# The opening of a diffusion layer: a conditioning product on four column strips, and squares summed by TensorE

## The chip, the cores and the metric

The kernel runs on one core of a Trainium2 chip. The metric is the device time of one execution in microseconds; for each version the median of its runs is compared. "The profile" is one execution recorded by the hardware profiler.

## The reference

One layer of a diffusion backbone over 512 latent tokens and 256 context tokens of 1024 features, all in float32. The layer is a feed-forward block, a token mixer (differential attention beside a short convolution) and a second feed-forward block. Only the beginning matters here:

```python
def rms_norm(x, g):
    xf = x.astype(jnp.float32)
    y = xf * lax.rsqrt(jnp.mean(xf * xf, axis=-1, keepdims=True) + EPS)
    return (y * g.astype(jnp.float32)).astype(x.dtype)

def modulate(x, shift, scale):
    return x * (1.0 + scale) + shift

def adaln(cond, w_mod, b_mod):
    m = jax.nn.silu(cond) @ w_mod + b_mod
    return jnp.split(m, N_MOD, axis=-1)

def swiglu(x, w_gate, w_up, w_down):
    return (jax.nn.silu(x @ w_gate) * (x @ w_up)) @ w_down

def ffn_sublayer(h, mods, pre_g, post_g, w_gate, w_up, w_down):
    shift, scale, gate = mods
    y = swiglu(modulate(rms_norm(h, pre_g), shift, scale), w_gate, w_up, w_down)
    return h + 0.5 * gate * rms_norm(y, post_g)
```

Two conditioning vectors (one for the latent tokens, one for the context) go through the same 1024 x 9216 matrix. Before the first gate and up products (1024 x 2816 each) can start, the kernel needs the first two of its nine parts, shift and scale, and one over the root mean square of every token.

## The kernel before

Features lie on partitions, tokens along the free axis. The 1024 features are 8 blocks `d` of 128 rows; the 2816 hidden features are 22 chunks `f`. A float32 product is mostly made as three float32r products of parts: `hi` (a cast by ScalarE, L64) and `lo` (a subtraction on VectorE or GpSimd, L69), so that `wx` (L94) issues hi x hi, hi x lo and lo x hi. A plain float32 product on TensorE shows as two records of the profile. All loads of the opening go out on one queue, SP's. The order on each engine is laid down by a planner at build time; it follows the order of the program text closely, with small swaps.

The opening (L236 to L374) runs in these steps:

- **Loads**, in order: the conditioning columns of blocks 0 to 2 (`load_mod`, L251, two halves of 512 KB for a block, 8 buffers), the latent tokens (8 x 256 KB), the context tokens (8 x 128 KB), the gate and up weights of hidden chunk 0 (2 x 512 KB, L271), and the conditioning columns of blocks 3 to 7.
- **Conditioning product** of a block (`mod_mm`): the two vectors are the stationary operand, the 256 columns (shift and scale of the block) move past, in 8 products over the 1024 rows. Blocks 0 to 3 (`NPLAIN = 4`) are made in plain float32 with a stationary operand of 4 columns. For blocks 4 to 7 `mod_split` first splits the columns into parts (two casts by ScalarE, a subtraction on VectorE and one on GpSimd), and 16 float32r products are made with 128 stationary columns, of which four hold the parts of the vectors.
- `mod_row` (L299) copies the resulting rows (4 x 256) out of PSUM; `mod_pick` turns them into columns with two small products against `pick`, which also adds the rows of the parts; `mod_col` (L310, L312) adds the bias and the gain.
- **Squares**: `sqadd` (L146) squares a block of tokens on ScalarE and adds it to one of two accumulators on VectorE or GpSimd. At the end `rstd_steps` (L109) makes four products for the latent tokens and two for the context, one for each 128 tokens, against a single column of ones; then comes the root (ScalarE), the reciprocal (VectorE), and a product of ones with a diagonal matrix for each 128 tokens (L123), which spreads the result over all partitions in PSUM: `pbl`, `pbc`.
- **Modulation** (`mod_x`, through `modulate`, L157): for the latent tokens and for the context each a multiplication on VectorE (L161, reading `pbl` or `pbc` in PSUM), a shift with a cast on ScalarE (L164) and the low part on VectorE (L165).
- **Gate and up products of chunk 0** (`gate_up_open`, L128): block by block, twelve products for each `d`, into four banks of PSUM. In the loop over blocks 3 to 7 each round has one conditioning product, the split of the next block's columns, the modulation of an earlier block, twelve gate and up products of that block, and the selection of the new block; the last three blocks follow.

After the opening, chunks 1 and on run through `gate_up1`: two loads of 512 KB, two splits, and 96 products for the two kinds of tokens. Between chunks VectorE sums the remaining conditioning products (`mod_unit`, L439), whose loads use the same queue and the same four buffers `wraw` as the weights.

Of the kernel before, what the change touches and what calls it, by code (L numbers as in the profile page):

```python
# [16 lines left out]
P = 128  # L17
DM = 1024
# [13 lines left out]
NFIRST = 3  # L32
NPLAIN = 4
# [8 lines left out]
class Builder:  # L42
# [51 lines left out]
    def wx(self, outs, w, xs, nk, ks=None):  # L94
        """outs[i] += W^T X_i over nk blocks; w = (hi, lo); xs[i](k) -> (hi, lo)."""
        whi, wlo = w
        for k in ks or range(nk):
            a = whi[:, k * P:(k + 1) * P]
            b = wlo[:, k * P:(k + 1) * P]
            for o, x in zip(outs, xs):  # L100
                xh, xl = x(k)
                self.mm(o, a, xh, k == 0, False)
                self.mm(o, a, xl, False, False)
            for o, x in zip(outs, xs):
                xh, xl = x(k)
                self.mm(o, b, xh, False, k == nk - 1)

# [1 line left out]
    def rstd_steps(self, pool, psp, tags, sq, T):  # L109
        nc = self.nc  # L110
        nb = T // P
        pst = self.t(psp, [P, 512], tags[0], bufs=tags[1])
        for b in range(nb):
            self.mm(pst[:, b:b + 1], sq[0][:, b * P:(b + 1) * P], self.ones[:, 0:1], True, True)
# [29 lines left out]
    def sqadd(self, pool, acc, src, d, T):  # L144
        """acc[0] collects the squares of the chunks; acc[1] holds some of them on the way."""
# [11 lines left out]
    def modulate(self, pool, h, pb, s, t, xh, xl, T, eng=None):  # L157
        """x = h * rstd * s + t, split into (xh, xl)."""
# [13 lines left out]
    # ------------------------------------------------------------------  # L172
    def build(self):
# [7 lines left out]
        # constants  # L181
# [25 lines left out]
        # per-feature columns  # L207
# [37 lines left out]
        sql, sqc = self.sqsum(sp, NT), self.sqsum(sp, NCX)  # L245
# [5 lines left out]
        def load_mod(d):  # L251
            wm[d] = []
            for hf in range(2):
                raw = self.t(sp, [P, DM], "wm", bufs=8)
# [13 lines left out]
        raws = []  # L268
        for i in range(2):
            raws.append(self.t(self.wp, [P, DM], "wraw", bufs=self.n_raw))  # L270
            nc.sync.dma_start(out=raws[i], in_=io["f1gu"][0, i])  # L271
        for d in range(NFIRST, ND):
            load_mod(d)

        def mod_split(d):
            wm[d] = [self.split(w, DM, [self.t(sp, [P, DM], tag, F32R, bufs=3)
                                        for tag in ("mhi", "mlo")], eng)
                     for w, eng in zip(wm[d], (None, nc.gpsimd))]
# [18 lines left out]
        def mod_row(pm):  # L297
            row = self.t(sp, [4, 256], "row", bufs=4)
            nc.scalar.copy(out=row, in_=pm[0:4, :256])  # L299
            return row  # L300

        def mod_pick(row, tag="pd"):
            pt = self.t(psf, [P, 512], tag, bufs=2)
            for m in range(2):
                self.mm(pt[:, 2 * m:2 * m + 2], row[:, m * P:(m + 1) * P], pick, True, True)
            return pt

        def mod_col(d, pt):
# [14 lines left out]
        condw = self.t(sp, [P, 8, P], "condw", F32R)  # L323
        condf = self.t(sp, [P, 8, 4], "condf")
        nc.gpsimd.memset(condw.bitcast(F32), 0.0)
        nc.gpsimd.memset(condf, 0.0)
        sc2 = sc.rearrange("p (k v) -> p k v", v=2)
        nc.vector.tensor_copy(out=condf[:, :, 0:2], in_=sc2)
        nc.vector.tensor_copy(out=condw[:, :, 0:2], in_=sc2)
        nc.vector.tensor_tensor(out=condw[:, :, 2:4], in0=sc2,  # L330
                                in1=condw[:, :, 0:2].bitcast(F32), op=ALU.subtract)
        pick = self.t(sp, [4, 2], "pick")
        nc.vector.tensor_tensor(out=pick, in0=self.ident[0:4, 0:2], in1=self.ident[0:4, 2:4],
                                op=ALU.add)

        rl = self.rstd_steps(sp, psf, ("pc", 2), sql, NT)
        rc = self.rstd_steps(sp, psf, ("pa", 2), sqc, NCX)
        rows, pms, pts = {}, {}, {}
        for d in range(NFIRST):
            pms[d] = mod_mm(d)  # L340
            if d:
                pts[d - 1] = mod_pick(rows.pop(d - 1), 'pb')
                mod_col(d - 1, pts.pop(d - 1))
            rows[d] = mod_row(pms.pop(d))
        for d in range(ND):
            self.sqadd(sp, sql, xt[d], d, NT)
        next(rl)
        pts[NFIRST - 1] = mod_pick(rows.pop(NFIRST - 1), 'pb')
        mod_col(NFIRST - 1, pts.pop(NFIRST - 1))
        for d in range(ND):  # L350
            self.sqadd(sp, sqc, ct[d], d, NCX)
        pbl = result(rl)
        next(rc)
        pbc = result(rc)
        gu0 = [self.split(raw, eng=eng) for raw, eng in zip(raws, (None, nc.gpsimd))]
        first = self.gate_up_open(psf, gu0, lat, cx)
        next(first)
        nx = 0
        for d in range(NFIRST, ND):
            pms[d] = mod_mm(d)  # L360
            if NPLAIN <= d + 1 < ND:
                mod_split(d + 1)
            rows[d] = mod_row(pms.pop(d))
            mod_x(nx)
            next(first)
            nx += 1
            pts[d] = mod_pick(rows.pop(d))
            mod_col(d, pts.pop(d))
        while nx < ND:
            mod_x(nx)  # L370
            next(first)
            nx += 1
# [13 lines left out]
        def gate_up1(f, part=(True, True), h=None, ps=None):  # L386
            """hidden chunk f of the latent and/or the context tokens."""
# [32 lines left out]
        def mod_unit():  # L420
            """conditioning products of two column pairs, summed over the row blocks."""
# [94 lines left out]
        # context stream: residual, norm, modulation for the mixer  # L516
# [44 lines left out]
        # keys and values of the context  # L561
# [501 lines left out]
def _blocks(w, nout):  # L1063
    """(K, nout*128) -> [nout][128 p][K/128 * 128]: column block o, row k*128+p."""
# [6 lines left out]
def _wide(w, n):  # L1071
    """(1024, n*256) -> [n][2][128 p][4*256]."""
# [40 lines left out]
def _rope():  # L1113
    """rotary tables, features on partitions; the sign of the rotation is in the sine."""
# [29 lines left out]
```

## Time and profile before

| | |
|---|---|
| median of 3 runs | 1675.19 us (1673.79 to 1679.26) |
| span of the profiled execution | 1675.4 us |
| TensorE busy | 1630.4 us, 97% |
| VectorE, ScalarE, GpSimd busy | 60%, 39%, 8% |
| moved by DMA | 232.85 MB, mean 139 GB/s |
| opening: first gate product of chunk 0 | issued at 35.11 us |
| opening: first product of chunk 1 | issued at 66.01 us |

In the profile PE is the stream of products of TensorE and PEld its loads of stationary operands, which run beside the products where they can. The two small letters of a row, out<-in, are names of the program: `pd<-wm,condf` is the plain conditioning product, `pd<-mhi,condw` the split one, `pb<-pick,row` the selection, `pc<-ones,sqacc` the sum of squares, `pa<-xhi,whi` a gate product. "128*4 128x256" after it is the stationary operand's size and the moving operand's. A bracket at the end of a row says how long the engine had been idle, and what ended it.

### The profile page before, as it was taken

Reading aid. Unit: us, or ns where it says so; the run is one execution under the profiler, and the core shown is the slowest. Engines: PE = TensorE matmul, PEld = TensorE weight load, DVE = VectorE, ACT = ScalarE, POOL = GpSimd, SP = SyncE. Lnnn points to the kernel's source line nnn. Section 1 sums busy time; section 2 is a strip of 40 time slices with the busy share of each in tenths; the row PEclk is TensorE's granted clock in tenths of the full one; section 3 lists DMA queues with packets and bytes.
Section 4 is the critical chain, followed back from the end, with each engine's and each line's share of the span. In section 5 each row is a group of like instructions: output and inputs, shape, how many; then the busy total and the mean of one; then the engine's idle time right before and its main releaser. Section 6 shows DMA issues by size and latency. Waiting matters only on the chain. (4 is left out here: it accounts for less than half of the span.)

```text
span 1675.4 us, 23611 instructions
## 1 busy us (share of the span) xinstructions
PE 1630.4 (97%) x9154; PEld 1410.8 (84%) x9154; DVE 1010.4 (60%) x1730; ACT 653.5 (39%) x1061; POOL 136.4 (8%) x120
## 2 busy tenths in 40 slices
PE   7999999999999998899999999999999999999996
PEld 4888888888888988889898888788889998888886
DVE  5975466447645699577777776473347843343345
ACT  5422222112211555355555555442247732223224
POOL 3100000000000145100000000000002100000003
PEclk8999999999999999999999999999999999999998
DMA  9343333235623447854545443733246743232321
GB/s 337 118 138 92 98 113 113 77 113 169 198 90 134 133 147 239 247 170 120 148 130 158 120 132 95 253 127 101 89 152 202 252 137 113 82 108 90 98 76 51
DMA packets 96400, 232.85 MB, mean 139 GB/s; under 512 B 11040, under 2 KB 35744, under 8 KB 96288
## 3 DMA queue, kind: packets, MB, share of 16 engines
q1 hardware_dynamic: 96288, 231.34, 43.6%
q8 instruction: 72, 1.18, 0.3%
q14 instruction: 40, 0.33, 0.1%
HBM read 201.94 MB, written 16.78 MB: 131 GB/s over the span
## 5 line engine op out<-in xcount | busy, mean ns | idle before, releaser
L64 ACT CAST whi<-wraw 128x1024 fp32r<-128x1024 f32 (+2 forms) x276 | 274.0, 994 | 624.3 <-PE pc L92 206.5
L69 DVE TENSOR_TENSOR wlo<-wraw,whi 128x1024 fp32r<-128x1024 f32 (+2 forms) x266 | 325.9, 1226 | 189.3 <-ACT whi L64 185.2
L92 PE MATMUL pa<-xhi,wlo 128*128 128x512 f32 (+1 forms) x528 | 196.6, 372 | 1.5 <-DVE wlo L69 1.5
L92 PE MATMUL pa<-xhi,whi 128*128 128x512 f32 (+1 forms) x528 | 197.2, 374 | 0.5 <-ACT ob L756 0.5
L92 PE MATMUL pa<-xlo,whi 128*128 128x512 f32 (+1 forms) x528 | 196.3, 372 | 0.9 <-DVE xlo L165 0.6
L92 PE MATMUL pb<-xhi,whi 128*128 128x512 f32 (+1 forms) x400 | 146.9, 367 | 0.0
L92 PE MATMUL pb<-xhi,wlo 128*128 128x512 f32 (+1 forms) x400 | 146.6, 366 | 0.0
L92 PE MATMUL pb<-xlo,whi 128*128 128x512 f32 (+1 forms) x400 | 146.0, 365 | 0.0
L92 PE MATMUL f<-xhi,whi 128*128 128x512 f32 x320 | 127.1, 397 | 0.0
L92 PE MATMUL f<-xhi,wlo 128*128 128x512 f32 x320 | 124.8, 390 | 0.0
L92 PE MATMUL f<-xlo,whi 128*128 128x512 f32 x320 | 124.5, 389 | 0.0
L92 PE MATMUL pd<-hh,whi 128*128 128x512 f32 x304 | 120.5, 396 | 0.9 <-ACT hh L64 0.9
L439 DVE SCALAR_TENSOR_TENSOR macc<-wraw,sc,macc 128x256 f32<-128x256 f32 x280 | 117.6, 480 | 5.8 <-DMA wraw<-wmod 4.8
L92 PE MATMUL pd<-hh,wlo 128*128 128x512 f32 x304 | 119.6, 394 | 0.0
L92 PE MATMUL pd<-hl,whi 128*128 128x512 f32 x304 | 118.8, 391 | 0.2 <-DVE hl L69 0.2
L92 PE MATMUL pc<-xchi,wlo 128*128 128x256 f32 x408 | 115.0, 282 | 2.1 <-DVE wlo L69 2.1
L92 PE MATMUL pc<-xclo,whi 128*128 128x256 f32 x408 | 114.9, 282 | 1.5 <-DVE xclo L165 1.5
L92 PE MATMUL pc<-xchi,whi 128*128 128x256 f32 x408 | 114.9, 282 | 1.3 <-DVE silu L69 1.3
L92 PEld LDWEIGHTS pa<-xhi,whi 128*128 128x128 f32 x528 | 99.5, 188 | 18.4 <-ACT ob L756 0.7
L92 PEld LDWEIGHTS pa<-xlo,whi 128*128 128x128 f32 x528 | 99.6, 189 | 12.8 <-DVE xlo L165 0.8
L92 PEld LDWEIGHTS pa<-xhi,wlo 128*128 128x128 f32 x528 | 99.9, 189 | 12.3 <-DVE wlo L69 1.7
L155 POOL TENSOR_TENSOR sqacc<-sqacc,sqt 128x256 f32<-128x256 f32 (+1 forms) x27 | 24.8, 918 | 894.8 <-ACT sqt L153 894.8
(293 smaller groups left out, 3348.6 us busy)
## 6 DMA issues: line engine op xcount, KB each, us to landing
wraw<-wmod SPq DMA_DIRECT2D x56, 512.0 KB, 3.6
wraw<-f2gu SPq DMA_DIRECT2D x56, 512.0 KB, 3.5
wraw<-f1gu SPq DMA_DIRECT2D x48, 512.0 KB, 3.9
wraw<-f1d SPq DMA_DIRECT2D x24, 384.0 KB, 3.2
wraw<-f2d SPq DMA_DIRECT2D x24, 384.0 KB, 3.2
wm<-wmod SPq DMA_DIRECT2D x16, 512.0 KB, 7.5
wraw<-wk SPq DMA_DIRECT2D x16, 512.0 KB, 4.3
wraw<-wv SPq DMA_DIRECT2D x16, 512.0 KB, 4.2
```

The costliest lines, as they stand in the source:

```text
L64: self.nc.scalar.copy(out=out, in_=src)
L69: (eng or self.nc.vector).tensor_tensor(out=out, in0=src, in1=hi.bitcast(F32), op=ALU.subtract)
L92: self.nc.tensor.matmul(out, lhsT=lhsT, rhs=rhs, start=start, stop=stop)
L155: eng.tensor_tensor(out=a, in0=a, in1=s, op=ALU.add)
L439: nc.vector.scalar_tensor_tensor(out=acc[:, i], in0=src, scalar=s, in1=acc[:, i], op0=ALU.mult, op1=ALU.add)
```

## The change

- The tokens are loaded first, then block 0's conditioning columns, the context tokens, the weights of chunk 0, and the conditioning columns of blocks 1 to 7. The buffers for these go from 8 to 14.
- All eight blocks of the conditioning product are made in plain float32. The stationary operand has 32 columns (two of them used). The eight products of a block are dealt out to four strips of 32 columns, which write to partitions 0, 32, 64 and 96 of one bank, two to each strip. The split of the columns is gone. The copy out of PSUM takes all 128 partitions, and the selection adds the four strips.
- The sums of squares are no longer accumulated by VectorE and GpSimd. Each block is squared by ScalarE or VectorE in turn, and TensorE sums it over partitions and over blocks: for each block four products (latent) or two (context) against a column of ones, into one bank.
- The context's modulation is a product on GpSimd (with `pbc` copied to SBUF), a scale and shift and a cast on ScalarE, and the low part on GpSimd.
- The low parts of the first weights are both made by VectorE. Blocks 0 and 1 are modulated ahead of the loop, which runs over blocks 2 to 7 and modulates each block in its own round.

```diff
-        for d in range(NFIRST):
-            load_mod(d)
         for d in range(ND):
             load_x(xt, io["xT"], NT, d)
+        load_mod(0)
         for d in range(ND):
             load_x(ct, io["ctxT"], NCX, d)
...
         def mod_mm(d):
             pm = self.t(psf, [P, 512], "pd", bufs=2)
-            if d < NPLAIN:
-                for kk in range(8):
-                    self.mm(pm[0:4, :256], condf[:, kk, :],
-                            wm[d][kk // 4][:, (kk % 4) * 256:(kk % 4) * 256 + 256],
-                            kk == 0, kk == 7)
-            else:
-                for kk in range(8):
-                    for i in range(2):
-                        w = wm[d][kk // 4][i]
-                        self.mm(pm[:, :256], condw[:, kk, :],
-                                w[:, (kk % 4) * 256:(kk % 4) * 256 + 256],
-                                kk + i == 0, kk + i == 8)
-            return pm
+            for kk in range(8):
+                j = 32 * (kk % 4)
+                self.mm(pm[j:j + 32, :256], condf[:, kk, :],
+                        wm[d][kk // 4][:, (kk % 4) * 256:(kk % 4) * 256 + 256],
+                        kk < 4, kk >= 4)
+            row = self.t(sp, [P, 256], "row", bufs=3)
+            nc.scalar.copy(out=row, in_=pm[:, :256])
+            return row
...
         def mod_x(d):
             self.modulate(sp, xt[d], pbl, s1[:, d, 0:1], mst[:, d, 0, 0:1], xhi[d], xlo[d], NT)
-            self.modulate(sp, ct[d], pbc[:, :NCX], s1[:, d, 1:2], mst[:, d, 1, 0:1],
-                          xchi[d], xclo[d], NCX)
+            u = self.t(sp, [P, NCX], "uctx", bufs=3)
+            nc.gpsimd.tensor_tensor(out=u, in0=ct[d], in1=pbc, op=ALU.mult)
+            nc.scalar.activation(u, u, AF.Identity, bias=mst[:, d, 1, 0:1], scale=s1[:, d, 1:2])
+            self.hi(xchi[d], u)
+            self.lo(xclo[d], u, xchi[d], nc.gpsimd)
...
+        def squares(src, T, tag):
+            pst = self.t(psf, [P, 512], tag, bufs=2)
+            for d in range(ND):
+                s = self.t(sp, [P, NT], "sqt", bufs=4)[:, :T]
+                if d % 2:
+                    nc.vector.tensor_tensor(out=s, in0=src[d], in1=src[d], op=ALU.mult)
+                else:
+                    nc.scalar.activation(s, src[d], AF.Square)
+                for b in range(T // P):
+                    nc.tensor.matmul(pst[:, b:b + 1], lhsT=s[:, b * P:(b + 1) * P],
+                                     rhs=self.ones[:, 0:1], start=d == 0 and b == 0,
+                                     stop=d == ND - 1, skip_group_check=True)
+            return pst
+
+        rows = {}
+        pst = squares(xt, NT, "pc")
+        rows[0] = mod_mm(0)
+        rl = self.rstd_steps(sp, psf, ("pc", 2), None, NT, pst)
         next(rl)
+        mod_col(0, rows.pop(0))
         pbl = result(rl)
+        pst = squares(ct, NCX, "pa")
+        rc = self.rstd_steps(sp, psf, ("pa", 2), None, NCX, pst)
         next(rc)
+        rows[1] = mod_mm(1)
+        pbc = self.t(sp, [P, NCX], "pbc")
+        nc.scalar.copy(out=pbc, in_=result(rc)[:, :NCX])
+        mod_x(0)
+        gu0 = [self.split(raw) for raw in raws]
         first = self.gate_up_open(psf, gu0, lat, cx)
         next(first)
+        mod_col(1, rows.pop(1))
+        mod_x(1)
+        for d in range(2, ND):
+            rows[d] = mod_mm(d)
             next(first)
+            mod_col(d, rows.pop(d))
+            mod_x(d)
+        next(first)
+        next(first)
         ps0 = result(first)
```

More of the change, by code (lines that the diff above doesn't have):

```diff
@@ L106, in wx, with rstd_steps @@
                 self.mm(o, b, xh, False, k == nk - 1)
-    def rstd_steps(self, pool, psp, tags, sq, T):
+    def rstd_steps(self, pool, psp, tags, sq, T, pst=None):
         nc = self.nc
         nb = T // P
-        pst = self.t(psp, [P, 512], tags[0], bufs=tags[1])
-        for b in range(nb):
-            self.mm(pst[:, b:b + 1], sq[0][:, b * P:(b + 1) * P], self.ones[:, 0:1], True, True)
+        if pst is None:
+            pst = self.t(psp, [P, 512], tags[0], bufs=tags[1])
+            for b in range(nb):
+                self.mm(pst[:, b:b + 1], sq[0][:, b * P:(b + 1) * P], self.ones[:, 0:1], True, True)
         r = self.t(pool, [P, 8], "rstd_s", bufs=2)
@@ L260, in load_x, with load_gu @@
             nc.sync.dma_start(out=dst[d], in_=src[d])
[L262 to L263 removed]
+        raws = []
+        def load_gu(i):
+            raws.append(self.t(self.wp, [P, DM], "wraw", bufs=self.n_raw))
+            nc.sync.dma_start(out=raws[i], in_=io["f1gu"][0, i])
         for d in range(ND):
             load_x(xt, io["xT"], NT, d)
+        load_mod(0)
         for d in range(ND):
             load_x(ct, io["ctxT"], NCX, d)
[L268 removed]
         for i in range(2):
[L270 to L271 removed]
@@ L272, in build @@
-        for d in range(NFIRST, ND):
+            load_gu(i)
+        for d in range(1, ND):
             load_mod(d)
[L275 to L278, printed above, removed]
         def mod_mm(d):
             pm = self.t(psf, [P, 512], "pd", bufs=2)
-            if d < NPLAIN:
-                for kk in range(8):
-                    self.mm(pm[0:4, :256], condf[:, kk, :],
-                            wm[d][kk // 4][:, (kk % 4) * 256:(kk % 4) * 256 + 256],
-                            kk == 0, kk == 7)
-            else:
-                for kk in range(8):
-                    for i in range(2):
-                        w = wm[d][kk // 4][i]
-                        self.mm(pm[:, :256], condw[:, kk, :],
-                                w[:, (kk % 4) * 256:(kk % 4) * 256 + 256],
-                                kk + i == 0, kk + i == 8)
-            return pm
@@ L304, in mod_pick, with mod_col @@
+            row = self.t(sp, [P, 256], "row", bufs=3)
+            nc.scalar.copy(out=row, in_=pm[:, :256])
+            return row
+        def mod_col(d, row):
+            pt = self.t(psf, [P, 512], "pd", bufs=2)
             for m in range(2):
                 self.mm(pt[:, 2 * m:2 * m + 2], row[:, m * P:(m + 1) * P], pick, True, True)
-            return pt
-        def mod_col(d, pt):
             for v in range(2):
@@ L321, in build @@
         nc.scalar.activation(sc.rearrange("p (k v) -> p v k", v=2),
                              vec[:, V_C:V_C + 16].rearrange("p (v k) -> p v k", v=2), AF.Silu)
-        condw = self.t(sp, [P, 8, P], "condw", F32R)
-        condf = self.t(sp, [P, 8, 4], "condf")
-        nc.gpsimd.memset(condw.bitcast(F32), 0.0)
+        condf = self.t(sp, [P, 8, 32], "condf")
         nc.gpsimd.memset(condf, 0.0)
-        sc2 = sc.rearrange("p (k v) -> p k v", v=2)
-        nc.vector.tensor_copy(out=condf[:, :, 0:2], in_=sc2)
@@ L329, in build @@
[L329 to L333, printed above, removed]
-                                op=ALU.add)
-        rl = self.rstd_steps(sp, psf, ("pc", 2), sql, NT)
-        rc = self.rstd_steps(sp, psf, ("pa", 2), sqc, NCX)
@@ L338, in build @@
[L338 to L346, printed above, removed]
+        nc.vector.tensor_copy(out=condf[:, :, 0:2], in_=sc.rearrange("p (k v) -> p k v", v=2))
+        pick = self.t(sp, [P, 2], "pick")
+        nc.vector.tensor_tensor(out=pick, in0=self.ident[:, 0:2], in1=self.ident[:, 32:34],
+                                op=ALU.add)
@@ new lines, in build @@
+        for j in (64, 96):
+            nc.vector.tensor_tensor(out=pick, in0=pick, in1=self.ident[:, j:j + 2], op=ALU.add)
+        def squares(src, T, tag):
[11 more added lines that the diff above has]
+            return pst
```

30 lines of the change are left out of this document (1 added, 29 removed).

## The prediction

> **What bounds the kernel now.** I read the page for the busy shares, then the opening in windows of ten microseconds, then its timeline engine by engine.
>
> ```profile
> span 1675.4 us, 23611 instructions
> PE 1630.4 (97%) x9154; PEld 1410.8 (84%) x9154; DVE 1010.4 (60%) x1730; ACT 653.5 (39%) x1061; POOL 136.4 (8%) x120
> ...
> 0.00:10.00 10.00, 4.29 (x12) 1.40 (x13) 0.99 (x9) 1.50 (x2) 1.88 (x9) 1.00 0.80 293
> 10.00:20.00 10.00, 9.23 (x46) 3.99 (x43) 3.79 (x8) 5.56 (x11) 2.53 (x2) 1.00 1.04 361
> 20.00:30.00 10.00, 6.67 (x28) 5.03 (x28) 7.55 (x24) 6.98 (x15) 4.07 (x3) 0.65 1.00 394
> 30.00:40.00 10.00, 9.92 (x50) 6.38 (x49) 7.75 (x16) 6.32 (x10) 2.77 (x2) 0.84 0.79 285
> ...
> 80.00:90.00 10.00, 10.00 (x58) 8.72 (x57) 9.01 (x21) 3.73 (x5) 0.00 (x0) 1.00 0.36 119
> ```
>
> The columns are window, length, busy time of PE, PEld, DVE, ACT and POOL, granted clock, DMA share, GB/s. TensorE is busy 97% of the span, and without a break once the opening is over (80 to 90 us), while VectorE has room there. So what the change does to the time is the shift of the moment at which TensorE gets to the second hidden chunk.
>
> ```profile
> 35.11 0.50 PE L92 MATMUL pa<-xhi,whi 128*128 128x512 f32 x1
> ...
> 65.90 0.28 PE L92 MATMUL pb<-xchi,wlo 128*128 128x256 f32 x1
> 66.01 0.39 PE L92 MATMUL pa<-xhi,whi 128*128 128x512 f32 x1
> ```
>
> The first chunk begins at 35.11, and its last product is issued at 65.90. The row at 66.01 is chunk 1. **66.0 us is the number to beat.** From chunk 1 on I cost nothing: the code is the same, and TensorE is the full engine there.
>
> Bytes do not set it. The opening loads 12.7 MB before and after (tokens 3.1, conditioning blocks 8.4, first weights 1.0, vectors 0.1). The four windows sum to 13.3 MB by 40 us, so the last conditioning block lands near 37 us in either version, and TensorE needs it far later (below).
>
> **The change, part by part.** All of it is on TensorE's queue, so I add up that queue.
>
> *Squares.* Before, VectorE and GpSimd add squares up and TensorE makes six one-column products (4+2). After, every one of 8 blocks goes to TensorE: 32 products for the latent tokens and 16 for the context, each with a 128-column stationary operand and one moving column.
>
> ```profile
> 21.33 0.97 PEld L92 LDWEIGHTS pc<-ones,sqacc 128*128 128x128 f32 x8 [1.44 <-DVE sqacc L155]
> ...
> 26.95 0.97 PEld L92 LDWEIGHTS pa<-ones,sqacc 128*128 128x128 f32 x4
> 27.80 0.55 PEld L92 LDWEIGHTS pc<-rstd_d,ones 128*128 128x128 f32 x2
> ```
>
> A float32 product is two load records (4 products, x8). At full clock eight take 0.97, about 0.11 apart. In the second row four fill 26.95 to 27.80, 0.21 apart. So a product costs 0.21 us at the full clock or 0.43 at the half. Which one?
>
> ```profile
> 5.71 8.84 PE L92 MATMUL pd<-wm,condf 128*4 128x256 f32 x32 [5.71 <-DMA wm<-wmod]
> ...
> 9.07 0.13 PEld L92 LDWEIGHTS pd<-wm,condf 128*4 128x4 f32 x1 [0.30 <-issue]
> 9.42 4.62 PEld L92 LDWEIGHTS pd<-wm,condf 128*4 128x4 f32 x22 [0.22 <-issue]
> ...
> 26.00:27.00 1.00, 1.00 (x5) 0.86 (x5) 0.98 (x5) 1.00 (x2) 0.00 (x0) 0.50 1.01 414
> ...
> 29.00:30.00 1.00, 1.00 (x4) 0.22 (x2) 0.96 (x3) 0.54 (x1) 1.00 (x1) 0.50 1.02 410
> ...
> 33.00:33.50 0.50, 0.50 (x3) 0.13 (x2) 0.50 (x2) 0.50 (x1) 0.00 (x0) 0.77 0.21 82
> ```
>
> The opening starts slow (a load of 0.13 behind a gap of 0.30 up to 9.07, so 0.43 apart; then 22 in 4.62 us, 0.21 apart), whatever the clock column prints there; 3.6 us of dense 256-column products released it. From 26 to 30 us TensorE is busy without a gap (the two rows left out read 1.00 as well), but partly on one-column and 128-column products, and the clock stays at 0.50 until 33.2. So a queue of loads with one moving column does not, by these rows, raise the clock. I take the half clock: 32 x 0.43 = 13.7 us and 16 x 0.43 = 6.8 us; the other end is 6.8 and 3.4.
>
> The Trainium skill (TensorE: Matmul & The Clock Gate, Part 1) says that the clock follows how busy TensorE was in windows of about 3.4 us. The 3.6 us agree; a busy window of loads that stays at 0.50 is what its words leave open.
>
> *First conditioning product.* Before: 8 float32 products a block for blocks 0 to 3 and 16 split ones for blocks 4 to 7. After: 8 float32 products a block, on four column strips.
>
> ```profile
> 15.83 3.62 PE L92 MATMUL pd<-wm,condf 128*4 128x256 f32 x16
> ...
> 53.54 0.60 PE L92 MATMUL pd<-pick,row 4*128 4x2 f32 x4
> 54.07 0.39 PE L92 MATMUL pd<-mhi,condw 128*128 128x256 f32 x1
> ...
> 56.07 0.39 PE L92 MATMUL pa<-xhi,whi 128*128 128x512 f32 x1
> ...
> 58.25 0.60 PE L92 MATMUL pd<-pick,row 4*128 4x2 f32 x4
> ```
>
> Eight float32 products are 16 records in about 3.4 us, 0.213 each. No row shows two strips at once. Ends: no overlap, 3.4; four strips wholly side by side, 4 x 0.213 = 0.85. Between them: if records start in program order, the second record of a product waits for its first, and only the next strip's first runs beside it: 8+1 steps, 9 x 0.213 = **1.9 us** (3.8 at half clock). I take this, since it is also nearest to the split form's 54.07 to 56.07, 2.0 us. So against blocks 4 to 7 nothing is gained; against 0 to 3 about 1.5 us each, at the same clock.
>
> The same page (Part 3) tells of three column strips that ran 2.38 times as fast, and that products start in strict order; no run here shows strips, and by 2.38 a block would be 1.4 us.
>
> *The round of one block* (selection product 0.5, conditioning product, gate and up products 2.1) is 58.25 - 53.54 = 4.7 us before. After: 1.9 + 2.1 + 0.5 and up to 0.4 for going into and out of the strip form (a 0.25 us issue gap stands before each selection product now) = 4.9.
>
> *Sum to chunk 0's first gate product, half clock.*
>
> ```profile
> 14.37 0.63 ACT L153 ACTIVATE sqt<-x 128x512 f32<-128x512 f32 x1
> ...
> 21.80 0.72 POOL L155 TENSOR_TENSOR sqacc<-sqacc,sqt 128x256 f32<-128x256 f32 x1 [2.67 <-ACT sqt L153]
> ...
> 51.81 0.39 PE L92 MATMUL pc<-xclo,whi 128*128 128x256 f32 x1 [1.47 <-DVE xclo L165]
> ```
>
> x first: the first 512 KB block is used at 5.71 now, and half as much should be there near 4.3; a square (0.63) later, 5.0. Squares 13.7: 18.7. Block 0: 3.8, 22.5. Four diagonal products (0.43) and the selection (0.9): 25.1. Context squares 6.8: 31.9. Block 1: 3.8, 35.7. Two diagonal products and a selection 1.7: 37.4. Block 2, 3.3 as the clock comes back: 40.7. The first context block is modulated by then (31.9, root and diagonals to 36.6, then a copy and four instructions of which two are such POOL ones of 0.72, an estimated 3 us). So it starts near 40.7 instead of 35.11. Then gates of block 0 2.3, selection 0.5, five rounds 24.5, gates of blocks 6 and 7 with the wait for the last modulation 4.7: **72.7**. If block 0's dense products lift the clock for a while, the squares behind them save 1 to 2 us: 71.5. Shift: +5.5.
>
> *What costs nothing.* The casts and subtractions of blocks 4 to 7 go from ACT, DVE and POOL. They lie beside TensorE's work except where it waited for them, longest at 51.81 (1.47 us, for xclo); the rounds above contain no such wait, so these go. The context's modulation moves to POOL (0.72 an operation by the row at 21.80, two a block) and ACT (three short ones): under 2 us of each against 4.9 a round. The second subtraction of the first weights moves from POOL to DVE, in time that TensorE spends on squares. More buffers: the last two of 16 conditioning loads wait on SP for block 0's product, and with them chunk 1's loads; that is over at 22.5 us, with blocks 3 to 6 still under way. If that cover went (product 0 after 33 us), the queue would run dry and chunk 1 be late.
>
> **Rivals.**
>
> (1) *Strips wholly side by side.* 0.85 instead of 1.9 at full clock, 1.7 instead of 3.8 at half. Up to the first gate product 2 x 2.1 + 1.6 = 5.8 less, but the modulated context is there at about 35.5, so 5.2 less; each of five rounds 1.0 less. 71.5 - 5.2 - 5.0 = about 62: 1671 to 1674. Against it: every float32 product is two records on the same strip, and PE's records stand in order in the timeline.
>
> (2) *Not slower: the squares run at full clock.* 10.2 us instead of 20.5, blocks 0 and 1 1.9 each less, diagonals and selections 2 less. 71.5 - 10.3 - 3.8 - 2 = 55.4, held up a little by the second and third conditioning blocks, which land near 20 and 23 us: 57, 1666; with (1) as well 1661. It decides where half-clock loads (0.43 a product) become full-clock ones. For it: the rows at 21.33 were at full clock. Against it: they came after 3.6 us of dense products, and 26 to 30 us.
>
> (3) *The strips do not overlap.* 3.4 us a block, 6.8 at half clock, less what the longer dense stretch gives back by lifting the clock. Up to the first gate product 3 to 5 more, each round 1.5 more: 71.5 + 4 + 7.5 = 83, 1692. Against it only that the strips hold different columns; nothing in the trace speaks for either.
>
> **How the numbers follow.** Forecast 0.42, 1681 with its own range 1677 to 1687; (1) 0.20; (2) 0.21; (3) 0.17. The sum is made against the profiled span of 1675.4, 0.2 above the median of the three runs. About 0.3%, 5 us, is what can be told from no change: below 1670.2 is faster, above 1680.2 slower. The forecast is slower in 0.28 and within it in 0.14; (1) is faster in 0.06 and within in 0.13, slower in 0.01; (2) faster in 0.20, same 0.01; (3) slower 0.16, same 0.01. Faster 0.26, same 0.29, slower 0.45. The range takes in the middle of (2) and of (3): 1662 to 1694.
>
> **What would show it.** Squares: load records of the one-column products 0.21 apart up to about 19 us, and a clock column that says 0.50 (or spacing that says it). Strips: the 16 records of a block spread over 1.9 us at full clock, not 0.9 or 3.4. The first gate product near 40, the second chunk near 71 to 73. Conditioning loads all landed by 38 us. Wrong at once if one-column loads stand 0.11 apart from the start, or if the plan puts the context squares behind gate products, or if another queue (POOL with the context's modulation, ACT with the row copies) makes TensorE wait inside a round.

## The result and the profile after

The changed kernel takes 1695.93 us (median of 4 runs, 1690.83 to 1698.59), the kernel before 1674.93 on the same chip: a ratio of 1.0119 (95% interval 1.0098 to 1.0140), 21 us slower. The prediction was 1681, with a range of 1662 to 1694.

The head of the page and the windows of the changed kernel, columns as before:

```profile
span 1694.4 us, 23764 instructions
PE 1646.4 (97%) x9238; PEld 1426.1 (84%) x9238; DVE 993.3 (59%) x1709; ACT 646.5 (38%) x1054; POOL 130.3 (8%) x126
```

```profile
10.00:20.00 10.00, 10.00 (x51) 9.17 (x50) 1.35 (x4) 2.48 (x4) 0.00 (x0) 1.00 1.04 383
20.00:30.00 10.00, 10.00 (x51) 8.97 (x51) 3.79 (x12) 2.13 (x5) 0.00 (x0) 1.00 1.03 410
...
40.00:50.00 10.00, 8.67 (x43) 5.22 (x43) 3.27 (x8) 3.63 (x7) 3.70 (x4) 0.57 0.07 26
...
60.00:70.00 10.00, 9.63 (x75) 5.93 (x68) 3.78 (x12) 4.39 (x9) 1.96 (x3) 1.00 0.16 41
70.00:80.00 10.00, 6.12 (x29) 4.13 (x28) 8.36 (x22) 6.51 (x9) 0.74 (x1) 0.95 0.14 49
80.00:90.00 10.00, 7.81 (x35) 6.71 (x36) 9.96 (x23) 2.69 (x3) 0.00 (x0) 0.71 0.59 207
```

The span grew by 19.0 us and TensorE's busy time by 16.0. Most of the loss is therefore not waiting but TensorE at work for longer: a busy share of 97% on both pages says nothing about the rate. From 10 to 30 us TensorE is full in both rows, and gets 51 records done in each ten; from 60 to 70 it gets 75 done in 9.63 us. Then there is a hole where there was none before: 6.12 and 7.81 busy out of 10 between 70 and 90 us, with VectorE nearly full.

TensorE's timeline of the changed kernel has the places:

```profile
4.81 13.78 PE L329 MATMUL pc<-ones,sqt 128*128 128x1 f32 x64 [4.81 <-ACT sqt L327]
...
24.28 6.12 PE L329 MATMUL pa<-ones,sqt 128*128 128x1 f32 x28
...
32.15 0.77 PE L90 MATMUL pa<-xhi,whi 128*128 128x512 f32 x1
...
39.39 0.64 PE L90 MATMUL pd<-wm,condf 128*32 128x256 f32 x8
41.11 0.39 PE L90 MATMUL pc<-xchi,whi 128*128 128x256 f32 x1 [1.07 <-ACT xchi L62]
...
46.94 1.08 PE L90 MATMUL pd<-wm,condf 128*32 128x256 f32 x8
...
52.85 0.64 PE L90 MATMUL pd<-wm,condf 128*32 128x256 f32 x8
...
57.40 0.64 PE L90 MATMUL pd<-wm,condf 128*32 128x256 f32 x8
...
74.75 0.39 PE L90 MATMUL pb<-xhi,wlo 128*128 128x512 f32 x1
76.29 0.50 PE L90 MATMUL pa<-xhi,whi 128*128 128x512 f32 x1 [1.16 <-ACT whi L62]
...
82.19 0.79 PE L90 MATMUL pa<-xhi,wlo 128*128 128x512 f32 x1 [4.21 <-DVE wlo L67]
```

Chunk 1 begins at 76.29 (66.01 before), stops 1.7 us later, and stands still for 4.21 us. A convenient mark of what each chunk costs is ScalarE's silu, which reads a chunk's finished gate product. Its rows for chunks 0 and 1, before and then after:

```profile
64.93 0.60 ACT L405 ACTIVATE silu<-pa 128x512 f32<-128x512 f32 x1 [0.55 <-PE pa L92]
...
74.52 0.60 ACT L405 ACTIVATE silu<-pa 128x512 f32<-128x512 f32 x1 [1.24 <-PE pa L92]
```

```profile
74.71 0.60 ACT L392 ACTIVATE silu<-pa 128x512 f32<-128x512 f32 x1 [0.27 <-PE pa L90]
91.72 0.60 ACT L392 ACTIVATE silu<-pa 128x512 f32<-128x512 f32 x1 [1.68 <-PE pa L90]
```

From the first to the second it was 9.6 us and is 17.0. The second silu is 17.2 us late, and at the later chunks up to 417 us this lag stays at 16.7 to 16.8. So all but a few microseconds is lost by 92 us: 9.8 by the end of chunk 0, 7.4 in chunk 1. The rest is at least partly in the view of waits: TensorE's longest stop for `hh`, the input of a down projection, grew by 2.2 us.

```profile
PE pd L92 <- ACT hh L64: 0.9, 1, 0.9
```

```profile
PE pd L90 <- ACT hh L62: 3.1, 1, 3.1
```

(The first fence is the kernel before, the second the changed one; 3.1 to 3.3 us stand in every kernel below but e4, with 1.6, and e10, with 0.9. These two alone keep the old conditioning product.)

What stopped chunk 1? It needs `wlo`, the low parts of its weights. These are VectorE's rows before, and then after:

```profile
58.64 1.22 DVE L69 TENSOR_TENSOR wlo<-wraw,whi 128x1024 fp32r<-128x1024 f32 x1
62.22 1.22 DVE L69 TENSOR_TENSOR wlo<-wraw,whi 128x1024 fp32r<-128x1024 f32 x1
```

```profile
79.34 1.66 DVE L426 SCALAR_TENSOR_TENSOR macc<-wraw,sc,macc 128x256 f32<-128x256 f32 x4
80.93 1.21 DVE L67 TENSOR_TENSOR wlo<-wraw,whi 128x1024 fp32r<-128x1024 f32 x1
82.06 0.47 DVE L426 SCALAR_TENSOR_TENSOR macc<-wraw,sc,macc 128x256 f32<-128x256 f32 x1
82.46 1.21 DVE L67 TENSOR_TENSOR wlo<-wraw,whi 128x1024 fp32r<-128x1024 f32 x1
```

The low parts need the high ones, which are ScalarE's casts. Before, these began at 56.80 and 59.40. After, both stand behind the silu of chunk 0:

```profile
75.20 1.99 ACT L62 CAST whi<-wraw 128x1024 fp32r<-128x1024 f32 x2
```

Before, chunk 1 was split inside the opening. After, the plan puts the casts behind chunk 0's silu and the low parts behind the later conditioning sums (`macc`, of `mod_unit`), which begin at 73.45. The weights are not late: both loads were issued by 35.9 us, and none into these buffers up to 100 us took over 10.2 us to land. So of the 7.4 us, 4.2 are the stop for `wlo` and 1.2 the wait for `whi` ahead of chunk 1. The rest, some 2, is by my estimate mostly the slower clock behind the stop (0.71 in the window from 80 to 90 us).

### The profile page after: what moved, and what is told of

Same layout as the page of the kernel before. It is cut to its first block, busy times and chain, and to the rows that moved or that the text cites. A ratio compares the mean times of both kernels' runs of the same rounds, so it can differ in the third digit from the quotient of the medians.

```text
span 1694.4 us, 23764 instructions
## 1 busy us (share of the span) xinstructions
PE 1646.4 (97%) x9238; PEld 1426.1 (84%) x9238; DVE 993.3 (59%) x1709; ACT 646.5 (38%) x1054; POOL 130.3 (8%) x126
## 5 line engine op out<-in xcount | busy, mean ns | idle before, releaser
L90 PEld LDWEIGHTS pa<-xhi,wlo 128*128 128x128 f32 x528 | 100.4, 190 | 17.3 <-DVE wlo L67 6.6
L90 PEld LDWEIGHTS pc<-xchi,whi 128*128 128x128 f32 x408 | 78.1, 191 | 18.4 <-ACT xchi L62 2.3
```

The source lines that it names most:

```text
L90: self.nc.tensor.matmul(out, lhsT=lhsT, rhs=rhs, start=start, stop=stop)
```

## The experiments

The theory from the two traces had two parts: the squares, 48 products with one moving column at half clock, and the late split of chunk 1. The rivals: the strips themselves, the new order of the loads, and TensorE doing work that other engines did before. Each was timed against runs of the kernel before on the same chip.

| kernel | time, us | ratio to before (95%) | silu of chunks 0 and 1, us | between |
|---|---|---|---|---|
| before | 1674.9 to 1676.6 | | 64.9, 74.5 | 9.6 |
| changed | 1695.93 | 1.0098 to 1.0140 | 74.7, 91.7 | 17.0 |
| e1 changed, squares added as before | 1682.02 | 1.0016 to 1.0041 | 62.0, 78.7 | 16.7 |
| e2 changed, early split of chunk 1 | 1686.39 | 1.0038 to 1.0084 | 76.1, 84.3 | 8.2 |
| e5 changed, both of these | 1676.40 | 0.9985 to 1.0009 | 61.4, 70.1 | 8.7 |
| e3 before, strips alone | 1680.26 | 1.0016 to 1.0042 | 60.9, 77.4 | 16.5 |
| e6 before, strips and early split | 1675.15 | 0.9975 to 1.0000 | 62.2, 70.3 | 8.1 |
| e4 before, one-column sums alone | 1696.32 | 1.0087 to 1.0130 | 79.6, 89.1 | 9.5 |
| e10 before, wide sums alone | 1681.50 | 1.0017 to 1.0041 | 69.2, 77.4 | 8.2 |
| e7 changed, wide sums | 1678.76 | 1.0009 to 1.0035 | 55.6, 73.8 | 18.2 |
| e9 changed, 128 columns moved | 1678.89 | 1.0004 to 1.0028 | 59.8, 77.1 | 17.3 |
| e11 changed, no strips | 1692.29 | 1.0077 to 1.0120 | 80.3, 89.3 | 9.0 |
| e8 changed, wide sums and early split | 1670.76 | 0.9954 to 0.9980 | 57.8, 66.5 | 8.8 |
| e12 changed, 128 columns and early split | 1671.33 | 0.9949 to 0.9978 | 60.9, 69.6 | 8.7 |

### One part undone: e1, e2, and both, e5

e1 adds the squares up on the engines again:

```diff
-        pst = squares(xt, NT, "pc")
+        for d in range(ND):
+            self.sqadd(sp, sql, xt[d], d, NT)
...
-        rl = self.rstd_steps(sp, psf, ("pc", 2), None, NT, pst)
+        rl = self.rstd_steps(sp, psf, ("pc", 2), sql, NT)
...
-        pst = squares(ct, NCX, "pa")
+        for d in range(ND):
+            self.sqadd(sp, sqc, ct[d], d, NCX)
```

> The changed kernel, with the sums of squares made as before the change (ScalarE squares, VectorE and GpSimd add up, six one-column products). Theory A, the loss comes from 48 one-column products at half clock on TensorE's queue (20.6 us there instead of about 2): the first gate product moves from 32 to about 22 us, the clock is back earlier, chunk 0's last product moves from 74.8 to 56-60 us, and the time from 1696 to 1676-1682. Theory B, the loss comes from the rounds (strips gone into and out of twice a block, the context's modulation on GpSimd and ScalarE within its own round): the squares only covered waits, and the time stays above 1690. Theory C, the loss is mainly the late parts of chunk 1's weights: the wait before its second product stays and the time is about 1690.

e2 loads and splits chunk 1's weights in the loop over blocks, and hands them to `gate_up1`:

```diff
+        pre = {}
         for d in range(2, ND):
+            if d == 5:
+                pre[1] = self.unit(io["f1gu"][1, 0]), self.unit(io["f1gu"][1, 1])
             rows[d] = mod_mm(d)
...
-                gu = self.unit(io["f1gu"][f, 0]), self.unit(io["f1gu"][f, 1])
+                gu = pre.pop(f, None) or (
+                    self.unit(io["f1gu"][f, 0]), self.unit(io["f1gu"][f, 1]))
```

> The changed kernel, with chunk 1's gate and up weights loaded and split ahead of block 5's round instead of after chunk 0. Theory A (the wait for chunk 1's low parts, 4.2 us, with the cast before it, 1.2, and the half clock after it, about 1.8, is a loss of its own): no gap of over 1 us between 74 and 84 us, 1689 (1687-1691). Rival (another wait takes its place, so that nothing is won): 1694-1697.

> The changed kernel with two edits at once: the squares added up on the engines as before (8 TensorE products for the sums instead of 48), and the weights of the second gate chunk loaded and split ahead of the sixth conditioning round. Theory: the loss is made of two separate things, the one-column products at half clock (13 us, first run of this study) and the late split of the second chunk (7 us, second run), and the strips themselves gain. Then both edits add up: ScalarE's silu of the second chunk near 71 us (78.7 with the adds alone, 91.7 in the changed kernel), no wait over 1 us in the second chunk, time 1672 us (1668 to 1676), a little under the kernel before. Rival, the two overlap (the early split's casts and subtractions stand on ScalarE and VectorE in the same rounds as the adds and only move the wait): silu near 78, time 1680 to 1684.

e1 takes 13.9 us off the changed kernel, e2 9.5, both 19.5. In e1 chunk 0 ends 12.7 us earlier and chunk 1 still takes 16.7. Theory A is right there about the squares, though chunk 0's last product comes at 62.0 and not by 60, and C about the stop, which stays at 4.23 us. In e2 it is the other way round: chunk 0 as late as ever, chunk 1 in 8.2, and the time 0.6 us under the range expected. So the two are separate, and e5 returns to the time of before, though not below it. Its second silu at 70.1 came as the theory had it, and 4.5 us ahead of before's; the time did not. That is the theory's miss here. Part of it may be the 3.1 us stop for `hh`, which e5 still shows. What makes up the rest is open.

### One part done: e3, e6, e4

e3 gives the kernel before the new `mod_mm`, with strips for all eight blocks, and drops `mod_split`. e6 adds the early split of e2 to it (at block 6).

> The kernel before, with only the conditioning product changed: all eight blocks in float32 on four strips, no split of the columns. Theory A (four strips run side by side, 0.43 us for half a block at full clock; the strips are a gain): block 3's product, 6.5 us with its pauses before, takes about 2.5, rounds take 4.5 instead of 4.7 and lose their waits for VectorE; chunk 0 ends near 59 instead of 66, 1668 (1664-1671). Theory B (going into and out of the strips eats the gain): 1674-1680.

> The kernel before with the strips alone (no split of the conditioning weights) and the second gate chunk's weights loaded and split ahead of the seventh block's round. Theory: the strips shorten each round by 0.7 us and the whole gain was given back by the late split (3.6 us wait and the clock lost with it); with the split early the second chunk's silu comes near 69 to 70 us (74.5 before, 77.4 with the strips alone), time 1669 to 1671. Rival, the strips gain nothing in the rounds and the opening is bound elsewhere (the loads, or VectorE's modulation of a block): silu at 74 to 77, time 1677 to 1680, as with the strips alone.

Both missed. In e3 chunk 0 does end 4.0 us earlier: the rounds take 4.0 us in place of 4.7. But chunk 1 takes 16.5, and TensorE's timeline of e3 has the same stop that the changed kernel has:

```profile
67.14 0.80 PE L92 MATMUL pa<-xhi,wlo 128*128 128x512 f32 x1 [3.58 <-DVE wlo L69]
```

The strips alone bring the late split with them. With the split early (e6) the second silu is at 70.3 as expected, yet the median gained no more than the edge of what the runs resolve. (Its trace is that of its fastest run, 1671.33 us, well under the median of 1675.15.)

e4 gives the kernel before the new `squares`, and nothing else.

> The kernel before, with only the squares changed: summed by TensorE as in the changed kernel (48 one-column products). Theory A: 11.5 to 13.7 us for the latent tokens and 6.8 for the context stand on TensorE's queue between block 2's product and the first gate product, which moves from 35 to 41-43; 1682 (1679-1686). Theory B (they lie in waits that are there anyway, and VectorE and GpSimd are relieved): 1672-1677.

1696.32: the whole loss of the change from one part, 14 us more than expected. TensorE's timeline of e4 says why:

```profile
19.43 3.79 PE L346 MATMUL pc<-ones,sqt 128*128 128x1 f32 x32
...
24.10 6.99 PE L346 MATMUL pc<-ones,sqt 128*128 128x1 f32 x32
...
30.95 6.97 PE L346 MATMUL pa<-ones,sqt 128*128 128x1 f32 x32
```

The three rows are the same work, 16 products in 32 records. The first follows the dense products of blocks 0 to 2 and runs at nearly twice the speed of the others. Then the speed halves, with TensorE busy throughout, and the clock column reads 0.65, 0.50 and 0.83 for 20 to 50 us.

### Does the single column cost the clock? e9, e7, e10

e9 changes what moves past each load of squares, 128 columns of ones in place of one. It does more arithmetic with the same 48 products and the same loads.

```diff
-                    nc.tensor.matmul(pst[:, b:b + 1], lhsT=s[:, b * P:(b + 1) * P],
-                                     rhs=self.ones[:, 0:1], start=d == 0 and b == 0,
+                    nc.tensor.matmul(pst[:, b * P:(b + 1) * P], lhsT=s[:, b * P:(b + 1) * P],
+                                     rhs=self.ones, start=d == 0 and b == 0,
                                      stop=d == ND - 1, skip_group_check=True)
-            return pst
+            return pst[:, 0:T:P]
```

> The changed kernel with one edit: each of the 48 products that sum the squares moves 128 columns of ones in place of one; the 128x128 loads of squares stay as they are, 48 of them, and the first of each 128 result columns is used. Theory, it is the lack of moving columns that holds the clock down: the clock rises after the first window, the latent sums take 8 to 10 us in place of 13.8 and the context's 3.5 to 4.5 in place of 6.1 though each product moves more, time 1685 to 1690. Rival, the weight loads themselves hold the clock down, whatever moves: 13.8 and 6 us or more, time 1695 to 1700.

1678.89: 17.0 us off the changed kernel, with more work done, and 6 us better than expected. In windows of one microsecond, counting the records of the squares alone, first the changed kernel and then e9:

```profile
9.00:10.00 1.00, 1.00 (x6) 1.00 (x6) 0.34 (x1) 0.00 (x0) 0.00 (x0) 1.00 1.05 424
10.00:11.00 1.00, 1.00 (x7) 1.00 (x6) 0.00 (x0) 0.63 (x1) 0.00 (x0) 1.00 1.03 422
11.00:12.00 1.00, 1.00 (x6) 1.00 (x7) 0.20 (x1) 0.00 (x0) 0.00 (x0) 1.00 0.99 370
```

```profile
9.00:10.00 1.00, 1.00 (x6) 1.00 (x6) 0.49 (x1) 0.00 (x0) 0.00 (x0) 1.00 1.02 410
10.00:11.00 1.00, 1.00 (x11) 1.00 (x10) 0.00 (x0) 0.63 (x1) 0.00 (x0) 1.00 1.03 418
11.00:12.00 1.00, 1.00 (x12) 1.00 (x11) 0.69 (x1) 0.00 (x0) 0.00 (x0) 1.00 0.99 379
```

The number to read is the count behind PE. Up to 10 us both do 6 records in a microsecond; from there e9 does 12, the changed kernel 6 to the end of its squares. The busy time is 1.00 in all rows, and so is the clock column, which at this early point shows no difference. The spacing of the records does, as at 9 us in the kernel before: 13.78 us for 64 records is 0.215 each, close to e4's third row (6.97 for 32, 0.218 each), where the clock column reads 0.50.

The latent sums themselves gain 3.9 us (13.78 to 9.92). More comes behind them, in what no longer runs at the low clock: the first gate product is issued at 22.59 in place of 32.15, and the silu of chunk 0 stands at 59.8 in place of 74.7. The plan moved some products as well (block 0's product is undivided in e9), which no run separates from this.

e7 and e10 sum the squares another way, ones as the stationary operand and 512 or 256 columns of squares moving, 16 products in all. The sums land on all partitions, and root and reciprocal run over the whole tile. e7 is the changed kernel with this, e10 the kernel before.

```diff
-                for b in range(T // P):
-                    nc.tensor.matmul(pst[:, b:b + 1], lhsT=s[:, b * P:(b + 1) * P],
-                                     rhs=self.ones[:, 0:1], start=d == 0 and b == 0,
-                                     stop=d == ND - 1, skip_group_check=True)
+                self.mm(pst[:, :T], self.ones, s, d == 0, d == ND - 1)
...
+            nc.scalar.activation(pb, pst[:, :T], AF.Sqrt, bias=self.eps, scale=1.0 / DM)
+            nc.vector.reciprocal(out=pb, in_=pb)
```

> The changed kernel with one edit: the squares are the moving operand, 512 or 256 columns wide, and a block of ones is the stationary one, so 16 products leave the sums on all partitions, and the square root and the reciprocal run over the whole tile; the products that spread them are gone. Theory, the one-column products cost their time because the clock never rises under them: with wide products TensorE is at clock 1.00 from the second window on, the sums take 13 to 15 us of records in place of 20 at half clock, the first chunk ends 6 to 12 us earlier, the late split of the second chunk stays (7 us), time 1683 to 1690. Rival, it is the occupancy of TensorE's queue alone: as many us of records as before, time 1693 to 1698; the unknown is the reciprocal over 128x512, which no run here shows.

> The kernel before with the squares summed by TensorE as 16 wide products with ones as the stationary operand, root and reciprocal over the whole tile, no other edit; the partner of the run that summed them as 48 one-column products (1696.3 us). Theory, that run lost its 20 us to the clock: here the windows from 20 to 40 us stand at 0.8 to 1.00 in place of 0.65 and 0.50, and the time is 1676 to 1684. Rival, putting the sums on TensorE at all is what costs, since they stand in its queue ahead of the first gate products: 1690 or more.

e10 has the sums on TensorE, ahead of the first gate products, as e4 has them, and is 14.8 us faster. Its clock reads 1.00 from 20 to 40 us, and its loss against the kernel before is 5 us, so sums on TensorE's queue need not cost 20. The other 15 of e4's loss are not the column count alone, since e10 also drops the products that spread the result and takes the reciprocal of a whole tile (3.35 us for 128x512). The test of the single column is e9, where nothing else is edited. e7 takes 1678.76, as e9 does, and 4 us less than the least expected.

### What the strips are worth: e11

```diff
-                j = 32 * (kk % 4)
-                self.mm(pm[j:j + 32, :256], condf[:, kk, :],
+                self.mm(pm[0:32, :256], condf[:, kk, :],
                         wm[d][kk // 4][:, (kk % 4) * 256:(kk % 4) * 256 + 256],
-                        kk < 4, kk >= 4)
+                        kk == 0, kk == 7)
```

> The changed kernel without the strips: all eight products of a block go into the same 32 columns one after the other, everything else as it is. Theory, the strips run side by side and are worth what they show: a block takes 3.4 us at full clock in place of 1.3 and two changes of mode of 0.8 together, so 1.2 to 1.5 us more in each of six rounds and up to 2 us each in blocks 0 and 1: 1703 to 1709. Rival, the strips are worth nothing beside their changes of mode: 1694 to 1698.

Neither: 1692.29, slightly less than with strips, and the two intervals overlap. In the changed kernel the strips gain nothing that the time shows. TensorE's timeline of e11:

```profile
18.50 5.24 PE L90 MATMUL pd<-wm,condf 128*32 128x256 f32 x16
...
25.18 1.50 PE L328 MATMUL pa<-ones,sqt 128*128 128x1 f32 x12
...
27.07 2.21 PE L328 MATMUL pa<-ones,sqt 128*128 128x1 f32 x16
...
63.37 3.64 PE L90 MATMUL pd<-wm,condf 128*32 128x256 f32 x16
...
69.76 3.64 PE L90 MATMUL pd<-wm,condf 128*32 128x256 f32 x16
```

And VectorE's:

```profile
64.53 1.22 DVE L67 TENSOR_TENSOR wlo<-wraw,whi 128x1024 fp32r<-128x1024 f32 x1
66.84 1.22 DVE L67 TENSOR_TENSOR wlo<-wraw,whi 128x1024 fp32r<-128x1024 f32 x1 [0.42 <-ACT whi L62]
79.14 0.61 DVE L422 TENSOR_SCALAR macc<-wraw,sc 128x256 f32<-128x256 f32 x2
```

A round takes 6.39 us (63.37 to 69.76) against 4.55 (52.85 to 57.40 in the changed kernel): the strips save 1.84 us in each, and chunk 0 ends 5.6 us earlier for it. Two things work against them. Without strips block 0's 16 records are a dense stretch of 5.24 us, in which the rate doubles (3 or 4 records a microsecond up to 22 us, then 7), so that most of the context's one-column squares run nearly twice as fast: 28 records in 3.7 us, against 6.12 in the changed kernel. (This is within the 5.6 us already.) And without strips the plan splits chunk 1 ahead of `macc`, though the rest of the program is the same: 9.0 us for chunk 1 in place of 17.0, no stop. In the table, every kernel with strips and without the early split takes 16.5 to 18.2 us for chunk 1, and every kernel without strips 8.2 to 9.6. So the late split comes from the strips, by way of the planner; which of its choices turns on them, no run shows. Nor was e12 run without strips. The nearest run is e6, where strips with an early split beat the kernel before by 1.2 us in the median, with an interval that reaches 1.

### Both repaired: e8, e12

e8 is e7 with the early split, e12 is e9 with it.

> The wide sums and the early load and split of the second gate chunk together, otherwise the changed kernel. Theory: the two gains add, 7 us under the run with the wide sums alone, 1675 to 1683. Rival: the early split meets the sums' reciprocal and the first blocks' modulation on VectorE, and the gain is under 3 us.

> The changed kernel with the two edits that each gave most back: 128 columns of ones past each load of squares, and the weights of the second gate chunk loaded and split ahead of the sixth conditioning round. Theory, the loss was these two things and nothing else: they add, the second chunk's silu comes near 68 to 69 us (77.1 with the columns alone), no wait over 1 us in the second chunk, time 1670 to 1674, under the kernel before and level with the wide sums with the early split (1670.8). Rival, the early split meets the rounds' casts on ScalarE and the gain is given back: silu at 73 or later, time 1675 to 1680.

1670.76 and 1671.33: e8 is 4 us under its range, and e12 within its own, with the second silu at 69.6 and no wait over 0.7 us in chunk 1. e12 is 24.6 us under the changed kernel. Of these e9 took 17.0 and the split then 7.6; in the other order, e2 took 9.5 and the columns then 15.1. Both kernels beat the one before by 5 to 6 us, with intervals clear of 1. Both keep the new order of the loads and the context's modulation on GpSimd and ScalarE, so these need no share in the loss; what they cost or gain by themselves was not run.

## Why the prediction was wrong, step by step

**The step that failed** is the sentence "From chunk 1 on I cost nothing: the code is the same". The code is the same and the plan is not. It cost 7.4 us in the trace of the changed kernel. In time, the early split gains 9.5 us from changed to e2, 8.0 from e7 to e8, 7.6 from e9 to e12, 5.6 from e1 to e5 and 5.1 from e3 to e6. With it the changed kernel takes 1686.4 (e2), at the upper end of the forecast's own range of 1677 to 1687. In the traces the shift is 19.0 us where the forecast had 5.5. Of the 13.5 between them, 3.4 stand ahead of chunk 0's last product (8.9 late), 8.3 from there to the second silu, and 1.8 later. The prediction had looked at chunk 1's loads, and at no engine that prepares its weights. VectorE's and ScalarE's rows for chunk 1 lay in the very stretch that was to change, at 57 to 63 us.

**Squares at half clock: right.** 13.78 us against 13.7 for the latent tokens, and 6.97 against 6.8 for the context (28 records in 6.12 us and four in 0.85). That one-column loads do not raise the clock was read from a busy stretch at 0.50; e9 shows it, and e4 that they do not hold it either. Rival (2) was thus dead as priced, but it named the place: what products that let the clock rise are worth there, e9 shows (17 us).

**Strips at 1.9 us a block: wrong in size.** Rival (1) was nearer (0.85): the strips run side by side. An undivided block in e9's timeline:

```profile
14.64 1.07 PE L90 MATMUL pd<-wm,condf 128*32 128x256 f32 x16
15.64 1.60 PE L329 MATMUL pa<-ones,sqt 128*128 128x128 f32 x12
```

16 records in 1.00 us to the next instruction, 3.57 in e11 (69.76 to 73.33): 3.6 times as fast. So the assumption behind the 1.9, that only the next strip's first record runs beside a product's second, does not hold. But in most rounds the plan cuts the block into two halves, with gate products between them, and each pays for going in and out. PEld's rows in the changed kernel:

```profile
52.85 0.16 PEld L90 LDWEIGHTS pd<-wm,condf 128*32 128x32 f32 x8 [0.36 <-issue]
53.41 0.19 PEld L90 LDWEIGHTS pb<-xlo,whi 128*128 128x128 f32 x1 [0.41 <-issue]
```

The loads stand still for 0.36 us ahead of a half and 0.41 behind it, the latter partly while its products run. By the Trainium skill (TensorEngine Tiling (Array Packing), Key Properties) a change of the tiling mode drains TensorE; these gaps fit that, but no run here separates a drain from other causes. A half is over in 0.57 us (52.85 to 53.42). So of a round's 4.55 us 1.1 are the strips, 0.4 the selection, 0.2 a wait for `xclo`, and 2.1 the gate and up products at the spacing that they had before. The 0.7 left over is an estimate for the pauses around the strips and the selection, where the prediction had up to 0.4. The round was put at 4.9, a little too long in all.

**First gate product near 40.7: early, at 32.15.** This is order and no gain. Up to the end of the context's squares the sum held, 30.4 against 31.9. Then it put blocks 1 and 2 ahead of the first gate product (8.8 us), and the plan issued them behind it, from 34.87 on. From there a case from the list of what would make the prediction wrong came true: TensorE waited for the context's modulation on GpSimd and ScalarE (the 1.07 at 41.11, and a 0.88 at 36.82). Its clock fell to 0.57 in the window from 40 to 50. The two rounds that begin at 39.39 and 46.94 take 7.55 and 5.91 us in place of 4.55, 4.4 us more together. So chunk 0's last product is issued at 74.75, against a forecast of 71.5 to 72.7 for its end.

**Bytes and hidden work.** The bytes do not set it, as said: once the squares have begun, no stop for a load stands in TensorE's timeline of the opening. The context's modulation was put at nothing, by comparing the busy time of GpSimd and ScalarE with a round. What counts is the chain from the selection to `xclo`, over several engines in turn: it makes TensorE wait as above, and in the later rounds for 0.17 to 0.19 us each.

**Rival (3), no overlap, 1692,** was close to the changed kernel's time by luck, since the strips do overlap. The kernel that does run without overlap, e11, takes 1692.29. There (3) is near the mark: 6.39 us a round against 6.4, chunk 1 begun at 80.78 against 83, and no late split.

What stays open: in e5 and e6 the second silu is over 4 us ahead of before's and the time by some 1 us at most in the medians. Some 2 us of that may be the longer stop for `hh`; the rest is open.

## What to carry to other kernels

When a stage is to get shorter, list what other engines do in its shadow for the next stage, and check that they still get it done; where a planner sets the order, a cheaper instruction is a change of order, so look at the plan of the next stage as well. Before moving a reduction to TensorE, ask how many columns move past each load: a one-column product held TensorE for the time of its load here, and cost the products behind it their clock. A busy share of 97% can hide a factor of two; count records per microsecond.

## What the runs showed of the hardware

- 48 float32 products with one moving column are slower than the same products with 128: 13.78 us against 9.92 for the first 32. Under one column TensorE counts as busy throughout in the trace and stays at 6 records a microsecond; under 128 columns, with the same loads, the rate doubles after 5 us.
- One-column products also lose a clock that was up: in e4 32 records took 3.79 us and the next 32 took 6.99. The Trainium skill (TensorE: Matmul & The Clock Gate, Part 1) has the clock follow how busy TensorE is in windows of some 3.4 us. The 3.79 us before it fell agree. In these rows TensorE shows as busy without a gap while the clock falls, so a busy share in the trace is not what keeps it up.
- Eight plain float32 products, two on each of four strips, run 3.6 times as fast as one after the other: 1.00 us in e9 against 3.57 in e11. The Trainium skill (TensorE: Matmul & The Clock Gate, Part 3) gives 2.38 for three strips, which no run here has.
